# A two-layer trunk on one core: modulation weights of the prologue in x's buffers, the shift shared by two engines, attention ahead of the substitution, half norms issued later

## The chip, the core and the metric

The kernel runs on one core of a Trainium2 chip. The core has five engines, each with its own in-order queue: TensorE (matrix products; PE in the profile, with PEld for its weight loads), VectorE (DVE), ScalarE (ACT), GpSimd (POOL) and SyncE (SP), from whose queue most transfers are issued. They work on SBUF (128 partitions) and on PSUM, where products accumulate in a few banks. The metric is device time in microseconds (us) of one execution, lower is better. Three timed runs of the kernel before gave 2611.18, 2620.76 and 2622.28 us; the median is 2620.76.

## What is computed

The reference is a decoder trunk of two layers on a sequence of 1024 rows of 1024 numbers in float32, one sequence. Each layer has a mixer and a SwiGLU feed-forward part, and a conditioning vector `c` gives shift, scale and gate of each. Layer 0's mixer is a gated delta rule with 8 heads of 128 numbers, layer 1's is latent attention. The change touches layer 0's first norm and its mixer:

```
mod = silu(c) @ ada_w[0] + ada_b[0]               # shift_m, scale_m, gate_m, ...
h = rmsnorm(x, norm_mix_g[0]) * (1 + scale_m) + shift_m
proj = h @ w_in                                   # q, k, v, gate z, decay a, beta b of 8 heads
q, k, v = silu(causal_conv(q, k, v)); q, k = l2norm(q), l2norm(k)
per head, by chunks:
    A = I + strict_lower(beta k k^T * decay)      # solved against k and v
    attn = (q k^T) * decay
    S = S * g_last + k_dec^T v_new;  o = q_dec S + attn v_new
o = rmsnorm(o, norm_g) * silu(z)
x = x + gate_m * (o @ w_out)
```

Then follow the feed-forward part, layer 1 in the same manner, and a last norm.

## The kernel before, in words

One large product is done as three float32r products of high and low parts (`mm3`, L195 to L202), so every weight and every activation is split: ScalarE casts the high part (L177), VectorE subtracts for the low one (L178). The program's text is a list of tile operations; a scheduler turns it into one in-order list for each engine. It takes what is ready by the text's order of priority and counts a tile as free when all its readers are done, so the position in the text and the number of buffers of a pool decide where an operation lands. Pools have `bufs` buffers for each name.

The prologue (`gdn_prologue`, L543 to L624) loads the eight row tiles of `x` (`xin`), norms and transposes them to `xT` (L604 to L611), and computes the columns `cols[1]` (scale) and `cols[0]` (shift) in two halves of 512 columns (`ada`, L562 to L602). A half takes four transfers of 512 KB for the scale and four for the shift, each into a buffer `raw` of two blocks of rows. VectorE multiplies and adds the eight blocks into `acc` (L582, L584) and TensorE sums `acc` over the partitions with a column of ones (L588); the second half's shift goes to TensorE alone instead (`on_pe`, L579). From these come `A`, `neg` and the modulated rows `hThi` (L597) and `hTlo` (L601), through `d`, which has the name `xin` too (L599, L600). The first head's K and Q projections follow (L647): 48 products for each half of the rows of `hT`, into four PSUM banks.

Then comes the loop over heads, written by hand as a string of steps (L685): K projects k and q, V projects v and z, A prepares `L` (beta k k^T with decay), B solves and computes the attention, R is the recurrence. While head h is in R, head h+1 is solved (B) and head h+2 is projected and its `L` prepared (K, A, V).

- B, `gdn_prep_b` (L403): ScalarE gathers the diagonal blocks into `Ld`, VectorE transposes them to `Lr` (L414), does 31 substitution steps of two operations each (`st` L421, `X` L423), and transposes back to `Xn` (L425). Then the attention `at` for two groups of four chunks: a decay `decT` (`gdn_decay`, L344: GpSimd, TensorE L355, ScalarE L357, GpSimd L359), four products of K and Q (L433) and a multiply by VectorE (L434). At last the blocks are joined to `U` (L435 to L472).
- R, `gdn_rec` (L475): eight chunks, one after the other. A chunk transposes k and v (L488, L489), multiplies the state `S` by k and q (L496, L497), forms the residual `r` (L499), multiplies by `U` (L506) to `y`, feeds the state (L511, L515) and the output row `on` (L518, L520), and ScalarE sums its squares (L524). After four chunks the half is normed (L526 to L541): `t` (L527, L529), the power -1/2 on GpSimd (`rpow`, L219, result `co`), the scaling of `on` (L532), four transposes (L537), the gate (L539) and the store to HBM.

Names that return below: `pj` is the PSUM tile of a projection, `wraw`, `whi` and `wlo` a weight as loaded and its two parts, `cacc` the convolution.

Of the kernel before, what the change touches and what calls it, by code (L numbers as in the profile page):

```python
# [9 lines left out]
F32 = mybir.dt.float32  # L10
# [4 lines left out]
ALU = mybir.AluOpType  # L15
# [4 lines left out]
P = 128  # L20
T = 1024
D = 1024
NT = T // P
KT = D // P
H = 8
FF = 2816
NF = FF // P
EPS = 1e-6
# [4 lines left out]
class Trunk:  # L33
# [369 lines left out]
    def gdn_prep_b(self, h, kq, pr):  # L403

        nc, v = self.nc, self.nc.vector
        K, Q, L = kq["KT"], kq["QT"], pr["L"]
        M, R8 = NT, 32 // NT

        Ld = self.gw.tile([P, 32, M], F32, name="Ld")
        for b in range(4):  # L410
            pb = slice(b * 32, b * 32 + 32)
            nc.scalar.copy(Ld[pb], L[pb, :, b * 32:b * 32 + 32].rearrange("p m j -> p j m"))
        Lr = self.gw.tile([P, 32, 32], F32, name="Lr")
# [10 lines left out]
        Xn = self.gw.tile([P, 8, R8, M], F32, name="Xn")  # L424
        v.transpose(out=Xn.rearrange("p c r m -> p c (r m)"), in_=X.rearrange("p i c -> p c i"))  # L425
        U = self.gb.tile([P, M, P], F32, name="U", bufs=2)
        at = self.gb.tile([P, M, P], F32, name="at", bufs=2)
        for qd in range(2):
            dec = self.gdn_decay(h, qd, True, "decT")
            pa = self.pc.tile([P, 4, P], F32, name="c")  # L430
            for i in range(4):
                cs = slice((qd * 4 + i) * P, (qd * 4 + i + 1) * P)
                nc.tensor.matmul(pa[:, i], K[:, cs], Q[:, cs], start=True, stop=True)  # L433
            v.tensor_tensor(out=at[:, qd * 4:qd * 4 + 4], in0=pa, in1=dec, op=ALU.mult)  # L434
# [40 lines left out]
    def gdn_rec(self, h, kq, pr):  # L475
# [4 lines left out]
        for half in range(2):  # L480
            on = self.gw.tile([P, 4, P], F32, name="on")
            ss = self.gs.tile([P, 4], F32, name="ss")
            for cc in range(4):
# [10 lines left out]
                if c > 0:  # L494
                    pks = self.pd.tile([P, 2, P], F32, name="d")
                    nc.tensor.matmul(pks[:, 0], K[:, cs], S, start=True, stop=True)  # L496
                    nc.tensor.matmul(pks[:, 1], Q[:, cs], S, start=True, stop=True)  # L497
                    r = self.gw.tile([P, P], F32, name="r", bufs=2)
                    v.scalar_tensor_tensor(out=r, in0=pks[:, 0], scalar=c2[:, c:c + 1], in1=vs,  # L499
                                           op0=ALU.mult, op1=ALU.add)  # L500
                    qs = self.gw.tile([P, P], F32, name="qs", bufs=2)
                    nc.scalar.activation(out=qs, in_=pks[:, 1], func=AF.Copy, scale=self.eg[:, g:g + 1])
                else:
                    r = vs
# [16 lines left out]
                else:  # L521
                    v.tensor_copy(on[:, cc], po)
                junk = self.gw.tile([P, P], BF16, name="junk2")
                nc.scalar.activation(out=junk, in_=on[:, cc], func=AF.Square, accum_out=ss[:, cc:cc + 1])  # L524

            t1 = self.gs.tile([P, 4], F32, name="t1")  # L526
            v.tensor_scalar(out=t1, in0=qq[:, half * 4:half * 4 + 4], scalar1=EPS, scalar2=P * EPS, op0=ALU.add,  # L527
                            op1=ALU.mult)
            v.scalar_tensor_tensor(out=t1, in0=ss, scalar=1.0 / P, in1=t1, op0=ALU.mult, op1=ALU.add)  # L529
            co = self.gs.tile([P, 4], F32, name="co")  # L530
            self.rpow(co, t1)
            v.tensor_tensor(out=on, in0=on, in1=co.rearrange("p (c o) -> p c o", o=1).broadcast_to([P, 4, P]),  # L532
                            op=ALU.mult)
            sl = slice(half * 512, half * 512 + 512)
            pt = self.pd.tile([P, 4, P], F32, name="d")
            for i in range(4):
                nc.tensor.transpose(pt[:, i], on[:, i], self.ident)  # L537
            oT = self.gw.tile([P, 512], F32, name="oT")
            v.scalar_tensor_tensor(out=oT, in0=pt.rearrange("p a b -> p (a b)"), scalar=self.ggdn, in1=Z[:, sl],  # L539
                                   op0=ALU.mult, op1=ALU.mult)  # L540
            nc.sync.dma_start(out=self.o_dram[:, h, sl], in_=oT)  # L541

    def gdn_prologue(self, hi, lo):  # L543
# [7 lines left out]
        with ExitStack() as st:  # L551
            pool = st.enter_context(self.tc.tile_pool(name="n1", bufs=2))
            xs = [pool.tile([P, D], F32, name="xin", bufs=8) for _ in range(NT)]
# [8 lines left out]
            def ada(half):  # L562

                for m in (1, 0):
                    pc = bank([P, 4])
                    on_pe = half == 1 and m == 0
                    if not on_pe:
                        acc = pool.tile([P, 512], F32, name="acc", bufs=2)
                    for b in range(4):
                        raw = pool.tile([P, 2, 512], F32, name="raw", bufs=5)  # L570
                        o = m * D + half * 512
                        nc.sync.dma_start(out=raw, in_=a["ada_w"][0, b * 256:(b + 1) * 256, o:o + 512]
                                          .rearrange("(b p) n -> p b n", p=P))
                        for i in range(2):
                            kt = 2 * b + i
                            c = self.cact[:, kt:kt + 1]
                            if on_pe:
                                for ct in range(4):
                                    nc.tensor.matmul(pc[:, ct:ct + 1], raw[:, i, ct * P:(ct + 1) * P], c,  # L579
                                                     start=(kt == ct == 0), stop=(kt == KT - 1 and ct == 3))  # L580
# [5 lines left out]
                    if not on_pe:  # L586
# [9 lines left out]
                for kt in range(half * 4, half * 4 + 4):  # L596
                    nc.scalar.activation(out=hi[:, kt], in_=xT[:, kt], func=AF.Identity, scale=A[:, kt:kt + 1],  # L597
                                         bias=cols[0][:, kt:kt + 1])
                    d = pool.tile([P, D], F32, name="xin", bufs=8)  # L599
# [26 lines left out]
    def gdn(self, right, outer):  # L626
# [5 lines left out]
        with ExitStack() as s2:  # L632
# [21 lines left out]
            self.gs = s2.enter_context(tc.tile_pool(name="gs", bufs=2))  # L654
            self.xs = self.gw.tile([P, 4, P], F32, name="Xs")
# [17 lines left out]
            def do(tok):  # L673
# [7 lines left out]
                if k == "G":  # L681
                    gate = self.gate_row(0, 2, self.gq_pool, "KT", 3)
                    self.pre = gate, self.out_w((0, 1), a["gdn_w_out"][0], gate)
                if k == "R" and h < H - 1: self.gdn_rec(h, kqv[h], pr[h])
            pre, loop, tail = "A0 V0 B0 K1 A1 V1", "B1 R0 K2 A2 V2", "B6 R5 K7 A7 V7 G0 B7 R6"  # L685
            for t in pre.split():
                do(t)
            for h in range(H - 1):
# [8 lines left out]
                if h in (2, 4):  # L697
# [4 lines left out]
                         lambda: self.gdn_rec(H - 1, kqv[H - 1], pr[H - 1]))  # L702
# [805 lines left out]
```

## Time and profile before

| What | Value |
|---|---|
| Median of three timed runs | 2620.76 us (2611.18 to 2622.28) |
| The profiled execution's own time | 2613.28 us |
| Its span in the profile | 2611.6 us |
| TensorE busy, share of the span | 2505.5 us, 96% |
| TensorE weight loads | 2058.1 us, 79% |
| VectorE busy | 1962.5 us, 75% |
| ScalarE busy | 1173.5 us, 45% |
| GpSimd busy | 171.5 us, 7% |
| Read from HBM, written | 247.16 MB, 78.14 MB |

The profile is that of one execution. Ends of pipelined products are modelled, so a busy TensorE is not one at its peak; the starts are the firmer numbers. PEclk is the granted clock of TensorE as a share of full speed (0.50 is 1.2 GHz, 1.00 is 2.4 GHz). The prologue ends near 76 us, the linear-attention stage near 752 us, where the output projection's rows begin.

### The profile page before, as it was taken

How to read it: one execution, taken by the hardware profiler on the slowest of the kernel's cores; microseconds unless marked ns; L12 is line 12 of the kernel's file. 1: busy time of each engine (PE TensorE's matmuls, PEld its weight loads, DVE VectorE, ACT ScalarE, POOL GpSimd, SP SyncE). 2: the span in 40 equal slices, each digit the busy share in tenths (PEclk: the TensorE clock that was granted, in tenths of full speed). 3: DMA queues.
4: the chain of work that ended last, by engine and by line, in shares of the span. 5: the costliest groups of instructions: out<-in, count | busy, mean ns of one | idle time of the engine just before them, and what ended most of it. 6: DMA issues, size and time to landing. Idle time of an engine off the chain costs nothing.

```text
span 2611.6 us, 35555 instructions
## 1 busy us (share of the span) xinstructions
PE 2505.5 (96%) x12757; PEld 2058.1 (79%) x12757; DVE 1962.5 (75%) x3748; ACT 1173.5 (45%) x2374; POOL 171.5 (7%) x322
## 2 busy tenths in 40 slices
PE   6999999999999999999999899999999999999998
PEld 5777777777778888888888798888779888887886
DVE  5787789888758888877586766668577777774778
ACT  5555454555465222322344665555283332332343
POOL 1211111221000000000000010000010000000000
PEclk8999999999999999999999999999999999999999
DMA  6111222331454544544945521112643332336634
GB/s 228 41 33 33 75 79 85 89 102 62 153 181 142 182 153 155 160 147 156 314 146 153 155 70 60 47 51 87 216 157 96 108 108 93 108 104 224 226 94 145
DMA packets 258705, 327.62 MB, mean 125 GB/s; under 512 B 17578, under 2 KB 176448, under 8 KB 258528
## 3 DMA queue, kind: packets, MB, share of 16 engines
q1 hardware_dynamic: 235840, 284.37, 34.7%
q10 hardware_dynamic: 22688, 40.97, 4.2%
q8 instruction: 101, 1.65, 0.3%
q14 instruction: 76, 0.62, 0.1%
HBM read 247.16 MB, written 78.14 MB: 125 GB/s over the span
## 4 chain that ended last, share of the span: by engine, by line
PE 77%; DVE 11%; ACT 4%; DMA 3%; issue 2%; POOL 2%; ACTq 0%; POOLq 0%; DVEq 0%; SPq 0%
PE pd L971 14%; PE nrm_p L202 14%; PE pj L202 14%; PE pd L202 10%; PE P L202 8%; PE pd L1288 3%; PE po L202 2%; DVE cacc L334 2%; PE pq L202 1%; PE tp L1331 1%; DVE X L423 1%; DVE st L421 1%; ACT Xs L441 1%; DVE wlo L178 1%; PE d L511 1%
## 5 line engine op out<-in xcount | busy, mean ns | idle before, releaser
L971 PE MATMUL pd<-wlo,gh 128*128 128x512 f32 x616 | 243.9, 396 | 2.5 <-DVE wlo L178 2.0
L971 PE MATMUL pd<-whi,gl 128*128 128x512 f32 x616 | 241.3, 393 | 0.9 <-DVE gl L178 0.9
L971 PE MATMUL pd<-whi,gh 128*128 128x512 f32 x616 | 236.9, 394 | 3.7 <-ACT gh L177 3.3
L202 PE MATMUL pj<-hThi,whi 128*128 128x512 f32 x480 | 197.0, 410 | 0.0
L202 PE MATMUL pj<-hThi,wlo 128*128 128x512 f32 x480 | 196.5, 409 | 0.0
L202 PE MATMUL pj<-hTlo,whi 128*128 128x512 f32 x480 | 196.0, 408 | 0.0
L177 ACT CAST gh<-wraw 128x1024 fp32r<-128x1024 f32 x84 | 82.3, 979 | 247.4 <-PE pd L971 209.2
L177 ACT CAST whi<-wraw 128x1024 fp32r<-128x1024 f32 (+3 forms) x105 | 100.8, 961 | 143.8 <-DMA wraw<-in_ffn_w_gate_dram 54.2
L178 DVE TENSOR_TENSOR gl<-wraw,gh 128x1024 fp32r<-128x1024 f32 x84 | 95.2, 1133 | 63.9 <-ACT gh L177 63.4
L971 PEld LDWEIGHTS pd<-wlo,gh 128*128 128x128 f32 x616 | 116.3, 189 | 33.3 <-DVE wlo L178 8.1
L219 POOL TENSOR_TENSOR nrm_r<-nrm_r,mh 128x1 f32<-128x1 f32 x56 | 37.4, 669 | 1585.3 <-DVE nrm_r L213 965.7
L971 PEld LDWEIGHTS pd<-whi,gh 128*128 128x128 f32 x616 | 116.2, 189 | 30.4 <-ACT gh L177 4.2
L178 DVE TENSOR_TENSOR wlo<-wraw,whi 128x1024 fp32r<-128x1024 f32 (+3 forms) x105 | 117.5, 1119 | 28.6 <-ACT whi L177 26.4
L971 PEld LDWEIGHTS pd<-whi,gl 128*128 128x128 f32 x616 | 116.3, 189 | 26.6 <-DVE gl L178 1.5
L202 PE MATMUL nrm_p<-T,xrow 128*128 128x512 f32 (+1 forms) x576 | 133.7, 387 | 0.0
L202 PE MATMUL nrm_p<-T,ow_hi 128*128 128x512 f32 (+1 forms) x600 | 132.0, 369 | 0.0
L202 PE MATMUL nrm_p<-T,ow_lo 128*128 128x512 f32 (+1 forms) x552 | 125.8, 376 | 0.0
L202 PEld LDWEIGHTS nrm_p<-T,xrow 128*128 128x128 f32 x576 | 105.3, 189 | 23.5
L202 PEld LDWEIGHTS nrm_p<-T,ow_hi 128*128 128x128 f32 x600 | 103.8, 189 | 20.6 <-ACT fh L791 0.2
L202 PEld LDWEIGHTS nrm_p<-T,ow_lo 128*128 128x128 f32 x552 | 98.0, 189 | 20.4
L334 DVE SCALAR_TENSOR_TENSOR cacc<-cr,cwc,cacc 128x512 f32<-128x512 f32 x144 | 108.5, 760 | 3.3 <-ACT cacc L332 2.8
L202 PEld LDWEIGHTS pj<-hTlo,whi 128*128 128x128 f32 x480 | 92.0, 192 | 15.4
(531 smaller groups left out, 6399.0 us busy)
## 6 DMA issues: line engine op xcount, KB each, us to landing
wraw<-in_ada_w_dram SPq DMA_DIRECT2D x80, 512.0 KB, 4.1
wraw<-in_ffn_w_gate_dram SPq DMA_DIRECT2D x44, 512.0 KB, 3.9
wraw<-in_ffn_w_up_dram SPq DMA_DIRECT2D x44, 512.0 KB, 4.4
gd_S<-sx ACTq DMA_DIRECT2D x88, 256.0 KB, 2.5
B<-in_ffn_w_down_dram SPq DMA_DIRECT2D x40, 512.0 KB, 6.8
wraw<-gd_S SPq DMA_DIRECT2D x40, 512.0 KB, 5.1
gd_A<-co ACTq DMA_DIRECT2D x66, 256.0 KB, 2.1
wraw<-in_gdn_w_in_dram SPq DMA_DIRECT2D x32, 512.0 KB, 4.6
```

The source lines that it names most:

```text
L177: nc.scalar.copy(hi, raw)
L178: nc.vector.tensor_tensor(out=lo, in0=raw, in1=hi.bitcast(F32), op=ALU.subtract)
L202: nc.tensor.matmul(out, l, r, start=(i == 0), stop=(i == len(seq) - 1))
L219: self.nc.gpsimd.tensor_tensor(out=out, in0=in_, in1=self.mh[:, 0:in_.shape[1]], op=ALU.pow)
L334: nc.vector.scalar_tensor_tensor(out=acc, in0=cr[:, j:j + 512], scalar=self.cw[:, j, ch:ch + 1], in1=acc, op0=ALU.mult, op1=ALU.add)
L421: v.tensor_tensor(out=t[:, 0:n], in0=Lr[:, j, j + 1:32].rearrange("p (i o) -> p i o", o=1).broadcast_to([P, n, 8]), in1=X[:, j:j + 1].broa ...
L423: v.tensor_tensor(out=X[:, j + 1:32], in0=X[:, j + 1:32], in1=t[:, 0:n], op=ALU.subtract)
L441: nc.scalar.copy(Xs[pb, :, b * 32:b * 32 + 32].rearrange("p m (r c) -> p m r c", c=8), Xn[pb, :, :, mh].rearrange("p c r m -> p m r c"))
L511: nc.tensor.matmul(psn, kd, y, start=True, stop=True)
L971: nc.tensor.matmul(acc[t], x[:, j, ts], y[:, j], start=(j0 + j == 0 and k == 0), stop=(j0 + j == NJ - 1 and k == 2))
L1288: nc.tensor.matmul(sc[:, 0:nm], q[:, ts], k[:, cs], start=(i == 0), stop=(i == 4 and not last))
L1331: nc.tensor.transpose(pt[:, kt - k0], pes[qi][:, kt * P:(kt + 1) * P], self.ident)
```

## The change

There are four edits, all in layer 0's first part.

1. The prologue's modulation weights lose their own buffers (`raw`, five) and are loaded under the name `xin`, which now has sixteen buffers instead of eight.
2. The shift is summed by both engines in both halves: even blocks of rows by VectorE into `acc`, odd ones by TensorE straight into PSUM, to which the product of `acc` with ones is added.
3. In B, the attention block stands ahead of the transposition to `Lr` and of the substitution instead of behind them; `Xn` takes the buffer `Ld`.
4. The norm of a half becomes a function of its own, `gdn_half`. The recurrence only notes the finished half; the norm is issued after the second chunk of the next half, or at a new step E of the string. `on` gets two buffers instead of one and `qs` one instead of two.

```diff
@@ gdn_prep_b
+        U = self.gb.tile([P, M, P], F32, name="U", bufs=2)
+        at = self.gb.tile([P, M, P], F32, name="at", bufs=2)
+        for qd in range(2):
+            dec = self.gdn_decay(h, qd, True, "decT")
+            pa = self.pc.tile([P, 4, P], F32, name="c")
+            for i in range(4):
+                cs = slice((qd * 4 + i) * P, (qd * 4 + i + 1) * P)
+                nc.tensor.matmul(pa[:, i], K[:, cs], Q[:, cs], start=True, stop=True)
+            v.tensor_tensor(out=at[:, qd * 4:qd * 4 + 4], in0=pa, in1=dec, op=ALU.mult)
         Lr = self.gw.tile([P, 32, 32], F32, name="Lr")
...
-        Xn = self.gw.tile([P, 8, R8, M], F32, name="Xn")
+        Xn = self.gw.tile([P, 32, M], F32, name="Ld").rearrange("p (c r) m -> p c r m", r=R8)
...
@@ gdn_rec
-            on = self.gw.tile([P, 4, P], F32, name="on")
+            on = self.gw.tile([P, 4, P], F32, name="on", bufs=2)
...
-                    qs = self.gw.tile([P, P], F32, name="qs", bufs=2)
+                    qs = self.gw.tile([P, P], F32, name="qs")
...
                 nc.scalar.activation(out=junk, in_=on[:, cc], func=AF.Square, accum_out=ss[:, cc:cc + 1])
-
-            t1 = self.gs.tile([P, 4], F32, name="t1")
...
+                if cc == 1:
+                    self.gdn_half()
+            self.gdn_end = (h, half, on, ss, qq, Z)
+
+    def gdn_half(self):
+
+        if self.gdn_end is None:
+            return
+        nc, v = self.nc, self.nc.vector
+        h, half, on, ss, qq, Z = self.gdn_end
+        self.gdn_end = None
+
+        t1 = self.gs.tile([P, 4], F32, name="t1")
...
@@ gdn_prologue
-            xs = [pool.tile([P, D], F32, name="xin", bufs=8) for _ in range(NT)]
+            xs = [pool.tile([P, D], F32, name="xin", bufs=16) for _ in range(NT)]
...
-                        raw = pool.tile([P, 2, 512], F32, name="raw", bufs=5)
+                        raw = pool.tile([P, D], F32, name="xin", bufs=16).rearrange("p (b n) -> p b n", b=2)
...
-                            if on_pe:
+                            if m == 0 and i == 1:
                                 for ct in range(4):
                                     nc.tensor.matmul(pc[:, ct:ct + 1], raw[:, i, ct * P:(ct + 1) * P], c,
-                                                     start=(kt == ct == 0), stop=(kt == KT - 1 and ct == 3))
+                                                     start=(kt == 1 and ct == 0), stop=False)
...
-                    if not on_pe:
-                        for ct in range(4):
-                            nc.tensor.matmul(pc[:, ct:ct + 1], acc[:, ct * P:(ct + 1) * P], self.ones[:, 0:1],
-                                             start=True, stop=True)
+                    for ct in range(4):
+                        nc.tensor.matmul(pc[:, ct:ct + 1], acc[:, ct * P:(ct + 1) * P], self.ones[:, 0:1],
+                                         start=(m == 1), stop=(m == 1 or ct == 3))
...
@@ gdn
+                if k == "E": self.gdn_half()
                 if k == "R" and h < H - 1: self.gdn_rec(h, kqv[h], pr[h])
-            pre, loop, tail = "A0 V0 B0 K1 A1 V1", "B1 R0 K2 A2 V2", "B6 R5 K7 A7 V7 G0 B7 R6"
+            pre, loop, tail = "A0 V0 B0 K1 A1 V1", "B1 R0 K2 E0 A2 V2", "B6 R5 K7 E0 A7 V7 G0 B7 R6 E0"
...
-                         lambda: self.gdn_rec(H - 1, kqv[H - 1], pr[H - 1]))
+                         lambda: (self.gdn_rec(H - 1, kqv[H - 1], pr[H - 1]), self.gdn_half()))
```

Lines of the kernel after are shifted: L655 is the first projections' product (L647 before), L605 and L608 the modulated rows (L597, L600), L540, L543 and L548 the norm's `t`, scaling and transposes (L529, L532, L537), L430 and L432 the substitution's steps (L421, L423).

How the engines' queues move is shown at three places. First ScalarE's list in the prologue, from the last copy of `xT` on, before:

```order
L611 COPY xT<-d 128x512
L177 CAST whi<-wraw 128x1024
L597 ACTIVATE hThi<-xT,col_0_161,Am_162 128x1024 x2
L600 ACTIVATE xin<-hThi,neg 128x1024 x2
L597 ACTIVATE hThi<-xT,col_0_161,Am_162 128x1024 x2
L600 ACTIVATE xin<-hThi,neg 128x1024 x2
L177 CAST whi<-wraw 128x1024
L597 ACTIVATE hThi<-xT,col_0_161,Am_162 128x1024 x2
```

And the same place after:

```order
L619 COPY xT<-d 128x512
L605 ACTIVATE hThi<-xT,col_0_161,Am_162 128x1024 x2
L608 ACTIVATE xin<-hThi,neg 128x1024 x2
L605 ACTIVATE hThi<-xT,col_0_161,Am_162 128x1024 x2
L608 ACTIVATE xin<-hThi,neg 128x1024 x2
L177 CAST whi<-wraw 128x1024 x2
L605 ACTIVATE hThi<-xT,col_0_161,Am_162 128x1024 x2
```

The cast of the first projection weight moved from ahead of the first modulated rows to behind all four of that half.

Second TensorE's list in head 2's recurrence, from the last projection products of the first half to the next chunk's products with the state, before:

```order
L202 MATMUL pj<-hThi,whi 128x512
L202 MATMUL pj<-hTlo,whi 128x512
L202 MATMUL pj<-hThi,wlo 128x512
L537 MATMUL d<-ident,on 128x128 x4
L488 MATMUL d<-ident,KT 128x128
L489 MATMUL d<-ident,VT 128x128
L202 MATMUL pj<-hThi,whi 128x512
L202 MATMUL pj<-hTlo,whi 128x512
L202 MATMUL pj<-hThi,wlo 128x512
L202 MATMUL pj<-hThi,whi 128x512
L496 MATMUL d<-S,KT 128x128
L497 MATMUL d<-S,QT 128x128
```

A chunk without the norm in a recurrence after, from the output row of one chunk to the next one's products with the state:

```order
L518 MATMUL d<-y,at 128x128
L202 MATMUL pj<-hThi,wlo 128x512
L202 MATMUL pj<-hThi,whi 128x512
L488 MATMUL d<-ident,KT 128x128
L489 MATMUL d<-ident,VT 128x128
L202 MATMUL pj<-hTlo,whi 128x512
L496 MATMUL d<-S,KT 128x128
L497 MATMUL d<-S,QT 128x128
```

At the half boundary the four transposes of the normed half, and the run of projection products ahead of them, no longer stand between one chunk and the next; two to five products do.

Third VectorE's list around the scaling (the `on` from `on` and `co`) of the same half of head 2, before:

```order
L515 SCALAR_TENSOR_TENSOR S<-S,eg_820,d 128x128
L423 TENSOR_TENSOR X<-X,st 128x48
L520 TENSOR_TENSOR on<-d,qs 128x128
L421 TENSOR_TENSOR st<-Lr,X 128x40
L334 SCALAR_TENSOR_TENSOR cacc<-cr,cwc,cacc 128x512
L423 TENSOR_TENSOR X<-X,st 128x40
L529 SCALAR_TENSOR_TENSOR t_2829<-ss,t_2829 128x4
L334 SCALAR_TENSOR_TENSOR cacc<-cr,cwc,cacc 128x512
L421 TENSOR_TENSOR st<-Lr,X 128x32
L532 TENSOR_TENSOR on<-on,co 128x512
```

And after:

```order
L499 SCALAR_TENSOR_TENSOR r<-d,c_1439,vs 128x128
L430 TENSOR_TENSOR st<-Lr,X 128x24
L540 SCALAR_TENSOR_TENSOR t_2888<-ss,t_2888 128x4
L432 TENSOR_TENSOR X<-X,st 128x24
L338 SCALAR_TENSOR_TENSOR KT<-KT,cacc 128x512
L430 TENSOR_TENSOR st<-Lr,X 128x16
L543 TENSOR_TENSOR on<-on,co 128x512
L432 TENSOR_TENSOR X<-X,st 128x16
L515 SCALAR_TENSOR_TENSOR S<-S,eg_825,d 128x128
```

The scaling stood behind the half's last update of the state and its output row; now it stands between the residual `r` of a later chunk and that chunk's update of `S`.

## Rows read from the trace of the kernel before

**Rows 1.** The page's first line.

```profile
span 2611.6 us, 35555 instructions
```

**Rows 2.** Windows: start:end, length, busy us and instructions by engine, granted clock, transfers.

```profile
core 0: us, PE busy (x) PEld busy (x) DVE busy (x) ACT busy (x) POOL busy (x), PEclk, DMA share, GB/s
0.00:76.00 76.00, 51.00 (x256) 42.33 (x257) 47.67 (x101) 46.67 (x65) 8.24 (x50) 0.89 0.63 204
...
250.00:350.00 100.00, 91.71 (x513) 74.13 (x511) 85.16 (x209) 50.66 (x132) 20.63 (x26) 0.97 0.27 79
```

**Rows 3.** Timeline, VectorE in the prologue: start, us, engine, line, operation, count.

```profile
30.78 4.69 DVE L584 SCALAR_TENSOR_TENSOR acc<-raw,cact,acc 128x512 f32<-128x512 f32 x6
...
64.00 2.47 DVE L601 SCALAR_TENSOR_TENSOR hTlo<-xT,Am,xin 128x1024 fp32r<-128x1024 f32 x2
```

**Rows 4.** Timeline, ScalarE in the prologue.

```profile
37.75 2.37 ACT L597 ACTIVATE hThi<-xT,col,Am 128x1024 fp32r<-128x1024 f32 x2 [1.81 <-DVE col L591]
...
44.37 2.18 ACT L600 ACTIVATE xin<-hThi,neg 128x1024 f32<-128x1024 f32 x2
...
60.18 2.37 ACT L597 ACTIVATE hThi<-xT,col,Am 128x1024 fp32r<-128x1024 f32 x2 [12.69 <-DVE Am L593]
```

**Rows 5.** Timeline, TensorE in the prologue.

```profile
42.53 0.79 PE L647 MATMUL pj<-hTlo,whi 128*128 128x512 f32 x1 [2.27 <-DVE hTlo L601]
...
47.22 1.84 PE L579 MATMUL d<-cact,raw 128*128 128x1 f32 x16
...
58.77 0.95 PE L588 MATMUL e<-ones,acc 128*128 128x1 f32 x8
...
64.94 0.62 PE L647 MATMUL pj<-hThi,whi 128*128 128x512 f32 x2
...
75.93 0.39 PE L202 MATMUL pj<-hThi,whi 128*128 128x512 f32 x1
```

**Rows 6.** Chain of waits, an undisturbed run of projection products.

```profile
555.40 13.30 PE pj L202 x58
```

**Rows 7.** Timeline, TensorE's products with U in heads 2 and 5, and the transposes.

```profile
271.41 0.46 PE L506 MATMUL d<-r,U 128*128 128x128 f32 x2
...
274.89 0.46 PE L506 MATMUL d<-r,U 128*128 128x128 f32 x2
...
280.27 0.66 PE L537 MATMUL d<-ident,on 128*128 128x128 f32 x4 [0.62 <-DVE on L532]
...
283.20 0.46 PE L506 MATMUL d<-r,U 128*128 128x128 f32 x2
...
509.70 0.46 PE L506 MATMUL d<-r,U 128*128 128x128 f32 x2
...
519.01 0.38 PE L506 MATMUL d<-r,U 128*128 128x128 f32 x2
```

**Rows 8.** Waits of TensorE, 150 to 752 us: total us, times, longest.

```profile
PE c L433 <- DVE at L434: 12.8, 5, 4.7
PE d L537 <- DVE on L532: 6.1, 10, 0.8
```

**Rows 9.** Waits of VectorE, 150 to 752 us.

```profile
DVE on L532 <- POOL co L219: 10.4, 11, 1.2
```

**Rows 10.** Timeline, VectorE: a substitution step near head 2's attention.

```profile
261.89 0.33 DVE L423 TENSOR_TENSOR X<-X,st 128x168 f32<-128x168 f32 x1
```

**Rows 11.** Windows: two stretches at half clock, as in rows 2.

```profile
261.60:268.40 6.80, 5.53 (x21) 5.14 (x22) 5.40 (x16) 1.99 (x7) 0.63 (x1) 0.50 0.25 77
...
654.10:660.90 6.80, 5.30 (x20) 4.67 (x21) 5.90 (x13) 2.62 (x7) 1.49 (x1) 0.50 0.55 186
```

**Rows 12.** The tile co (ns: min/median/max), and a scaling in VectorE's timeline.

```profile
L219 POOL TENSOR_TENSOR co<-t,mh x16: 1006/1019/1955, 199.2 to 736.5; 128x4 f32<-128x4 f32 x16
...
279.52 0.69 DVE L532 TENSOR_TENSOR on<-on,co 128x512 f32<-128x512 f32 x1 [0.90 <-POOL co L219]
```

**Rows 13.** Timeline, ScalarE: one of the prologue's table loads.

```profile
69.01 1.28 ACT L1101 ACT_TABLE_LOAD   x1
```

More of the change, by code (lines that the diff above doesn't have):

```diff
@@ L423, in gdn_prep_b @@
             v.tensor_tensor(out=X[:, j + 1:32], in0=X[:, j + 1:32], in1=t[:, 0:n], op=ALU.subtract)
-        Xn = self.gw.tile([P, 8, R8, M], F32, name="Xn")
+        Xn = self.gw.tile([P, 32, M], F32, name="Ld").rearrange("p (c r) m -> p c r m", r=R8)
         v.transpose(out=Xn.rearrange("p c r m -> p c (r m)"), in_=X.rearrange("p i c -> p c i"))
[L426 to L434, printed above, removed]
         for m0 in range(0, M, 4):
@@ L524, in gdn_rec @@
                 nc.scalar.activation(out=junk, in_=on[:, cc], func=AF.Square, accum_out=ss[:, cc:cc + 1])
-            t1 = self.gs.tile([P, 4], F32, name="t1")
[L527 to L540, printed above, removed]
@@ L541, in gdn_rec @@
-            nc.sync.dma_start(out=self.o_dram[:, h, sl], in_=oT)
+                if cc == 1:
[8 more added lines that the diff above has]
+        t1 = self.gs.tile([P, 4], F32, name="t1")
+        v.tensor_scalar(out=t1, in0=qq[:, half * 4:half * 4 + 4], scalar1=EPS, scalar2=P * EPS, op0=ALU.add,
+                        op1=ALU.mult)
+        v.scalar_tensor_tensor(out=t1, in0=ss, scalar=1.0 / P, in1=t1, op0=ALU.mult, op1=ALU.add)
+        co = self.gs.tile([P, 4], F32, name="co")
+        self.rpow(co, t1)
+        v.tensor_tensor(out=on, in0=on, in1=co.rearrange("p (c o) -> p c o", o=1).broadcast_to([P, 4, P]),
+                        op=ALU.mult)
+        sl = slice(half * 512, half * 512 + 512)
+        pt = self.pd.tile([P, 4, P], F32, name="d")
+        for i in range(4):
+            nc.tensor.transpose(pt[:, i], on[:, i], self.ident)
+        oT = self.gw.tile([P, 512], F32, name="oT")
+        v.scalar_tensor_tensor(out=oT, in0=pt.rearrange("p a b -> p (a b)"), scalar=self.ggdn, in1=Z[:, sl],
+                               op0=ALU.mult, op1=ALU.mult)
+        nc.sync.dma_start(out=self.o_dram[:, h, sl], in_=oT)
@@ L565, in ada @@
                     pc = bank([P, 4])
-                    on_pe = half == 1 and m == 0
-                    if not on_pe:
-                        acc = pool.tile([P, 512], F32, name="acc", bufs=2)
+                    acc = pool.tile([P, 512], F32, name="acc", bufs=2)
                     for b in range(4):
-                        raw = pool.tile([P, 2, 512], F32, name="raw", bufs=5)
+                        raw = pool.tile([P, D], F32, name="xin", bufs=16).rearrange("p (b n) -> p b n", b=2)
                         o = m * D + half * 512
@@ L585, in ada @@
                                                        op1=ALU.add)
-                    if not on_pe:
-                        for ct in range(4):
-                            nc.tensor.matmul(pc[:, ct:ct + 1], acc[:, ct * P:(ct + 1) * P], self.ones[:, 0:1],
-                                             start=True, stop=True)
+                    for ct in range(4):
+                        nc.tensor.matmul(pc[:, ct:ct + 1], acc[:, ct * P:(ct + 1) * P], self.ones[:, 0:1],
+                                         start=(m == 1), stop=(m == 1 or ct == 3))
                     hs = slice(half * 4, half * 4 + 4)
@@ L598, in ada @@
                                          bias=cols[0][:, kt:kt + 1])
-                    d = pool.tile([P, D], F32, name="xin", bufs=8)
+                    d = pool.tile([P, D], F32, name="xin", bufs=16)
                     nc.scalar.activation(out=d, in_=hi[:, kt].bitcast(F32), func=AF.Identity, bias=neg[:, kt:kt + 1])
@@ L654, in gdn @@
             self.gs = s2.enter_context(tc.tile_pool(name="gs", bufs=2))
+            self.gdn_end = None
             self.xs = self.gw.tile([P, 4, P], F32, name="Xs")
```

## The prediction

> **What bounds the kernel now.** I began with the two builds' instruction orders: from the end of the linear-attention stage on, the rows of all five engines are the same, so only the first 752 us of the 2611.6 us span [rows 1] can move. The windows came next [rows 2]: in the prologue (0 to 76 us) no engine is full (TensorE 51.00 of 76) and transfers run at 204 GB/s; in the stage's loop TensorE shows 91.71 us of 100 busy and VectorE 85.16, both near full and neither full. The reader is to see two coupled in-order queues: a stall in one is partly filled by the other. Then I read the prologue's timeline [rows 3 to 5], the recurrence around a half boundary [rows 6, 7], and the waits of TensorE and VectorE over 150 to 752 us [rows 8, 9].
>
> A normal chunk of the recurrence takes 274.89 - 271.41 = 3.48 us from one product with `U` to the next. A chunk at a half boundary takes 283.20 - 274.89 = 8.31 in head 2 and 519.01 - 509.70 = 9.31 in head 5 [rows 7], mean 8.8: there the power on POOL, the scaling on VectorE and four transposes (from 280.27, after 0.62 us idle) stand in TensorE's queue ahead of the next chunk. The time is not empty: by the order, fourteen or fifteen projection products stand before the transposes.
>
> **The change part by part.** *Prologue.* The same sixteen transfers of 512 KB are fetched. The shift's four even blocks of rows go to VectorE and the four odd ones to TensorE, in both halves. First half: eight multiply-adds become four. The last six before took 4.69 us, 0.78 each [rows 3]; four fewer is 3.1 us, plus some 0.6 of waiting inside the longer run, so the first modulated row (37.75 [rows 4]) starts near 34. Then the order decides. Before, ScalarE rounds the first projection weight ahead of the modulated rows; after, both weight casts stand behind all eight of those operations. These take 44.37 + 2.18 - 37.75 = 8.8 us [rows 4], so the first product waits until 34 + 8.8 + one cast of 1.0 = 43.8. Before, TensorE's products ran from 42.53 on [rows 5]. The 3.7 us gained are spent, and 1.3 more.
>
> Second half: the shift is now half on VectorE, and its closing product stands in TensorE's queue behind all 48 products of the first half. From 43.8 I add 48 products at 0.229 (13.30 / 58 [rows 6]) = 11.0; two groups of shift products at 1.84 [rows 5], where four stood in this stretch, = 3.7; two closing groups of 0.95 [rows 5] = 1.9; and 2.7 because the first dozen still run at half clock, at twice 0.229. This gives 63.1, and with the adds behind it the second half's rows start at 63.4 instead of 60.18 [rows 4]. Before, TensorE had products of the first half until 64.94 [rows 5] and saw no gap; now its queue is empty. VectorE's first low part ended at 64.00 + 1.24 = 65.2, 5.0 after that start [rows 3, 4]; now it ends at 68.4, and the 44 products behind it end at 68.4 + 44 x 0.229 = 78.5, where the next projection began at 75.93 [rows 5]. With a short stretch at half clock behind the gap: **+3 us**. Bounds: -4 (the early start survives) and +5. That all weights are fetched ahead I price at nothing: by the 34 us above they have landed, and the queues in front of their users are longer.
>
> *Attention ahead of the substitution.* The text moves it ahead of the 31 substitution steps. In the orders it hardly moves: TensorE still meets these products behind the next head's V projection (57 to 69 products before, 48 to 74 after). In heads 1, 3, 4 and 5 VectorE has one to three fewer substitution pairs in front of the first `at`, some 0.7 us a pair (a step there 0.33 [rows 10]); in head 7 two more. TensorE's waits for `at` are 12.8 us in five places [rows 8]. I take 1.4 off in three of them: **-4 us**. Bounds: 0, and all 12.8 with the two stretches at half clock behind the longest waits (6.8 each, granted clock 0.50 [rows 11], half of which is lost), -19.6.
>
> *Half norms later.* The same instructions, moved: the norm of a half is issued after the second chunk of the next half, or at the points E of the schedule. A boundary chunk on TensorE holds 23 products (5.3), four transposes (0.5) and some 1.3 us of small products (by the starts in a normal chunk): 7.1 of 8.8, 1.7 lost. A normal chunk holds eight (1.8) and 1.3: 3.1 of 3.48, 0.4 lost. The difference, 1.3 us at eight first boundaries, is 10.4. At the eight ends of a head other products stand ready, and I give these only 1 for what is left of the 6.1 us wait for the scaled half [rows 8], and 2 for the last head's shorter tail: **-13.5 us.** What is late next: VectorE. The scaling now stands between the residual `r` and the update of the state `S`, on the recurrence itself. It waits for POOL's power, 1.019 us median, with one to four short operations as cover, and takes 0.69 itself [rows 12]. Queued behind it are the update and, through it, TensorE's next two products with `S`. In front of these TensorE has some four to eight projection products, four transposes and two more, about 2.7 us, so a delay of 0.8 to 1.7 is covered; uncovered it costs up to 16 x 1.7 = 27. Bounds: -42, if the 5.3 us by which a boundary exceeds a normal chunk vanished eight times, and +27. I take the value nearest to the boundary rows, as each end needs all places to fall one way. The single `qs` buffer costs nothing: its reader stands right behind the update, ahead of the next chunk's writer; were it late, up to eight chunks of each head would wait a fraction of a microsecond. Of the table loads two fall away, 1.28 each [rows 13], beside waits of ScalarE: nothing, and at most -2.6.
>
> Sum: 3 - 4 - 13.5 = -14.5 us on the profiled execution's own 2613.28 us: 2598.8. That execution is 7.5 us below the median of the three timed runs (2620.76) and 2.1 above their lowest; I add half of the 7.5 for where a new median would lie: **2602.5 us**.
>
> **Rivals.** *Larger gain.* The waits for `at` go too, with their half-clock stretches: 19.6 instead of 4, so 2587. For it: these are the longest single waits, up to 4.7 [rows 8]. Against it: the orders leave the products where they were.
>
> *No change.* VectorE is the real bound: with 85 us of 100 busy [rows 2] and the same instructions, what TensorE gains at the boundary comes back as a wait for VectorE elsewhere. The prologue's +3 stays and the loop gives 0: 2613.3 + 3 + 3.7 = 2620. For it: VectorE's wait for the power, 10.4 us in eleven places [rows 9], stays, as little stands between the power and its user. Against it: 15 us in 100 of VectorE are idle.
>
> *Slower: the norm sits on the recurrence.* At each of the 16 norms the state's update waits for power and scaling. This decides from the point where the delay passes the 2.7 us that TensorE holds ready, or where the recurrence and not TensorE's stream sets the pace. Price: 16 x 1.7 = 27, less the 8 x 1.1 that the boundaries save beyond their products, prologue +5: +23, so 2640. For it: the power has run up to 1.955 us [rows 12]; at that length the delay reaches 2.6. Against it: the median is 1.019. The Trainium skill (GPSIMD Engine Reference, section Key points) says that GpSimd shares its SBUF interfaces with VectorE and contends with VectorE instructions that have two SBUF inputs; the substitution's steps are such, and the deferred power runs among them. The spread from 1.006 to 1.955 [rows 12] agrees with a contention; by that rule the long value would be the usual one and the time this rival's, by the median row it is the forecast's.
>
> **How the numbers follow.** Forecast 0.45, own range 2592 to 2612; larger gain 0.17; no change 0.26; slower 0.12. What a measurement can tell from no change is 0.5%, 13 us: below 2607.7 or above 2633.9. Faster: 0.36 of the forecast's 0.45, all of the larger gain, 0.01 of no change: 0.54. Slower: 0.11, most of the last rival. Within: 0.35. The range leaves out about half of each outer rival: 2582 to 2625.
>
> **What the profile will show.** Right: boundary chunks of 3.5 to 4.5 us from one product with `U` to the next; TensorE's wait for the scaled half near 0; the prologue's first product near 44, ScalarE's second batch of rows near 63, the next projection near 78.5; waits for `at` of some 9 us; the stage's end near 737 instead of 752. Wrong: a first product before 41 (the cast was not the gate); VectorE's wait for the power well over 10.4 with TensorE idle behind a late `S` (the slower rival); boundaries gone but the stage's end unmoved, with new waits at the V projection or behind the substitution (no change).

## The result, and the profile after

The kernel after takes 2643.18 us, the median of 13 runs (2624.76 to 2646.66), beside 2621.24 for the kernel before: the ratio is 1.008, interval 1.0063 to 1.0097. It is slower by 22 us, where 18 us less had been forecast.

The profiled execution took 2624.76 us and was the shortest of the thirteen; eight took 2643 to 2647. This profile therefore holds only part of the loss, and is read first for what it does show. Its span is 2623.0 us. Two stretches of 676 us follow, the loop over heads after and the same length before (columns as in [rows 2]; the x counts are instructions):

```profile
85.00:761.00 676.00, 638.23 (x3527) 505.14 (x3526) 552.90 (x1452) 350.39 (x914) 118.30 (x160) 0.98 0.27 81
```

```profile
76.00:752.00 676.00, 638.48 (x3522) 506.77 (x3521) 552.54 (x1451) 349.02 (x911) 117.21 (x159) 0.98 0.27 81
```

The loop gives next to nothing back: the same busy time and, within five, the same number of TensorE instructions in 676 us. From the first product of the next projection to the first one of the output projection's rows it takes 674.3 us after (86.6 to 760.9) and 675.9 before (75.9 to 751.8). What this profile loses lies ahead of the loop, 10.7 us, and, by two stretches at half clock that are 3.4 us longer and one that is new, behind it, some 2.3 us.

**The prologue after**, by ScalarE's, TensorE's and VectorE's timelines (start, us, engine, line, operation):

```profile
24.19 0.30 ACTq L1079 DMA_DIRECT2D pi<-in_positions_dram  x1
...
39.29 2.37 ACT L605 ACTIVATE hThi<-xT,col,Am 128x1024 fp32r<-128x1024 f32 x2 [7.76 <-DVE col L599]
...
47.98 1.97 ACT L177 CAST whi<-wraw 128x1024 fp32r<-128x1024 f32 x2
69.21 2.38 ACT L605 ACTIVATE hThi<-xT,col,Am 128x1024 fp32r<-128x1024 f32 x2 [19.26 <-DVE col L599]
```

```profile
33.14 4.15 PE L588 MATMUL d<-cact,xin 128*128 128x1 f32 x26
37.15 1.84 PE L596 MATMUL d<-ones,acc 128*128 128x1 f32 x8
49.06 0.79 PE L655 MATMUL pj<-hThi,whi 128*128 128x512 f32 x1 [10.07 <-ACT whi L177]
...
86.59 0.39 PE L202 MATMUL pj<-hThi,whi 128*128 128x512 f32 x1
```

```profile
28.87 0.22 DVE L1081 CAST pf<-pi 8x128 f32<-8x128 int32 x1 [2.08 <-DMA pi<-in_positions_dram]
```

Against [rows 4, 5]: the first rows start at 39.29 instead of 37.75, the first product at 49.06 (bulk at 42.53 before), the second half's rows at 69.21 instead of 60.18, the next projection at 86.59 instead of 75.93.

**The half boundary after**, TensorE's products with `U` in head 2 (against [rows 7]), then the last one of head 2 and the first of head 3; below them the same pair before:

```profile
282.57 0.46 PE L506 MATMUL d<-r,U 128*128 128x128 f32 x2
286.07 0.46 PE L506 MATMUL d<-r,U 128*128 128x128 f32 x2
290.13 0.46 PE L506 MATMUL d<-r,U 128*128 128x128 f32 x2
...
309.60 0.38 PE L506 MATMUL d<-r,U 128*128 128x128 f32 x2
350.02 0.38 PE L506 MATMUL d<-vs,U 128*128 128x128 f32 x2
```

```profile
303.94 0.38 PE L506 MATMUL d<-r,U 128*128 128x128 f32 x2
340.38 0.39 PE L506 MATMUL d<-vs,U 128*128 128x128 f32 x2
```

The boundary chunk is 290.13 - 286.07 = 4.06 us where it was 8.31. But from one recurrence to the next it is now 40.42 us where it was 36.44: projection products that left the recurrence stand there (130 in this stretch, 113 before; the boundary chunk has 11 instead of 23). TensorE's waits over 150 to 762 us after (us, times, longest), and the row of before that answers to the second:

```profile
PE c L420 <- DVE at L421: 15.1, 7, 4.6
PE e L447 <- DVE U L443: 6.2, 4, 2.4
PE d L548 <- DVE on L543: 2.8, 4, 1.0
PE d L488 <- DVE S L515: 2.2, 6, 0.5
```

```profile
PE e L447 <- DVE U L443: 3.4, 3, 2.2
```

The wait for the scaled half fell from 6.1 [rows 8] to 2.8; waits for `S` (2.2) and for `U` (2.8 more) came, and those for `at` rose from 12.8 [rows 8] to 15.1. All of TensorE's waits from 76 to 762 us add up to 37.1 us in both profiles.

### The profile page after: what moved, and what is told of

It is laid out like the page before. It is cut to its first block, busy times and chain, and to the rows that moved or that the text cites. A ratio compares the mean times of both kernels' runs of the same rounds, so it can differ in the third digit from the quotient of the medians.

```text
span 2623.0 us, 35565 instructions
## 1 busy us (share of the span) xinstructions
PE 2511.0 (96%) x12765; PEld 2060.2 (79%) x12765; DVE 1960.9 (75%) x3748; ACT 1170.7 (45%) x2372; POOL 172.2 (7%) x322
## 4 chain that ended last, share of the span: by engine, by line
PE 78%; DVE 11%; ACT 4%; DMA 4%; issue 2%; POOL 2%; SPq 0%; ACTq 0%; POOLq 0%; DVEq 0%
PE pd L981 15%; PE nrm_p L202 14%; PE pj L202 14%; PE pd L202 10%; PE P L202 8%; PE pd L1298 3%; PE po L202 2%; PE pq L202 1%; DVE cacc L334 1%; PE tp L1341 1%; DVE wlo L178 1%; DVE st L430 1%; DVE X L432 1%; ACT Xs L441 1%; PE pj L655 1%
```

## Where the other 20 us are: a second profile of the kernel after

The kernel was run again, unchanged, beside its parts.

> The kernel after, unchanged, timed beside its parts. Every theory expects a ratio near 1.008 to the kernel before. What it is to tell: the profiled execution after took 2624.76 us and was the fastest of thirteen, most took some 2645. If the 20 us between are stretches at half clock, a profile of a slower execution shows 40 us more at 0.50 than the first profile, and shows in which stage.

Measured: 2645.0 us, ratio 1.0072 (1.0044 to 1.0100). The profiled execution took 2648.7. Two stretches at the same times in both profiles, first the shorter execution's, then this one's (PEclk, the granted clock, is the third number from the end; in the second stretch the shorter execution is 7 us ahead in its work):

```profile
178.10:202.00 23.90, 22.32 (x146) 17.89 (x146) 16.37 (x35) 12.69 (x32) 4.19 (x6) 0.93 0.08 23
239.50:263.40 23.90, 23.90 (x131) 19.57 (x131) 17.93 (x55) 11.00 (x31) 3.52 (x6) 1.00 0.11 32
```

```profile
178.10:202.00 23.90, 23.90 (x102) 19.59 (x102) 10.06 (x17) 10.12 (x21) 5.31 (x6) 0.50 0.09 23
239.50:263.40 23.90, 23.90 (x108) 20.04 (x108) 11.12 (x38) 7.79 (x23) 2.24 (x3) 0.50 0.12 34
```

Twice 23.9 us passed at 1.2 GHz. The order of instructions is the same, and so are the waits at the two joins: TensorE's first product with `U` of heads 1 and 2, at the joins at the end of B (h = 0 and 1 in the code). They are, in the shorter execution and in this one:

```profile
177.14 1.10 PE L447 MATMUL e<-U,L 128*128 128x64 f32 x8 [2.38 <-DVE U L443]
231.55 1.10 PE L447 MATMUL e<-U,L 128*128 128x64 f32 x8 [1.92 <-DVE U L443]
```

```profile
177.41 1.37 PE L447 MATMUL e<-U,L 128*128 128x64 f32 x8 [2.36 <-DVE U L443]
238.89 1.42 PE L447 MATMUL e<-U,L 128*128 128x64 f32 x8 [1.91 <-DVE U L443]
```

In the first, half clock lasted 3.4 us from 178.2 and 3.4 from 232.8; in the second 23.9 and 23.9. The second execution has 54.7 us more at half clock in all (130.7 against 76.0 by the profile's clock, counted behind 30 us), half of which is 27, and is 24 us longer.

Each run also tells its mean granted clock. From it comes a second number for each kernel: the run's time less (1 - clock) x span, which counts half of each stretch at 1.2 GHz as lost. It is rough (the clock is given to 0.001, 2.6 us, and a stretch in which TensorE waits costs less), but it parts the two causes. Below, medians; "full-clock" is the mean of that number over the runs. The ratio is to runs of the kernel before in the same session, so it is no quotient of these medians.

| Kernel | runs | us | ratio to before (interval) | clock | full-clock us |
|---|---|---|---|---|---|
| before | 107 | 2621 | | 0.984 | 2579 |
| after (both rows of runs) | 19 | 2644 | 1.008, 1.0072 | 0.977 | 2583 |
| p_only: prologue alone | 12 | 2622 | 1.0009 (0.9995 to 1.0022) | 0.986 | 2584.5 |
| h_only: half norms alone | 12 | 2621.5 | 0.9991 (0.9977 to 1.0006) | 0.984 | 2579 |
| a_only: attention ahead alone | 12 | 2614 | 0.9993 (0.9974 to 1.0013) | 0.986 | 2577 |
| ha: half norms and attention | 12 | 2624 | 1.0017 (0.9998 to 1.0037) | 0.984 | 2581 |
| ph: prologue and half norms | 12 | 2629 | 1.0022 (1.0008 to 1.0037) | 0.982 | 2583 |
| pa: prologue and attention | 12 | 2627 | 1.0028 (1.0013 to 1.0042) | 0.982 | 2581 |

So the loss is some 4 us of work and waits and some 19 of clock: (0.984 - 0.977) x 2640 = 18.5. In the two profiles above the same reckoning gave 27 where the times differ by 24, so the clock's part may be nearer 16 and the rest nearer 6. No single edit has it.

## The experiments

**One edit or two at a time.** Each kernel is the kernel before with parts of the diff shown above.

```diff
 p_only   edits 1 and 2        ha   edits 3 and 4
 h_only   edit 4 (Xn in Ld)    ph   edits 1, 2 and 4
 a_only   edit 3               pa   edits 1, 2 and 3
```

> The kernel before with the changed prologue alone. Theory 1 (the loss is the prologue: in the trace after, its next projection starts some 9 us late, and the loop gives nothing back): ratio 1.004 to 1.008, next projection near 85 us instead of 75.93. Theory 2 (the norm on the recurrence, in the loop, makes the loss): 1.000 to 1.002.

> The kernel after with the prologue of before: attention ahead and half norms later, without the first two edits. Theory 1: ratio 0.997 to 1.002, so the loop's edits are worth nothing. Theory 2: 1.004 to 1.008. The prediction's sum without its prologue term: 0.993.

> The kernel before with the half norms alone (prologue and the attention's place as before; Xn in the buffer Ld, as after). Theory 1: 0.997 to 1.002, boundary chunks near 4 us but the stage's end unmoved. Theory 2: 1.004 to 1.008. The prediction's term: 0.995.

> The kernel after with the attention back behind the substitution (prologue and half norms as after). Theory 3 (the loss is half clock: TensorE's wait of 2.4 us for U at head 1's join and a new one of 1.9 at head 2's let the clock fall, and in most executions it then stays down through the whole join, 23.9 us each time, as a second profile of the kernel after shows): the wait at head 2's join comes with the attention's new place, so this kernel has at most one long stretch: ratio 0.999 to 1.003. Rival (the prologue's 10 us simply come on top of the loop's edits): 1.004 to 1.008.

> The kernel after with the norms of before (prologue and attention ahead of the substitution as after). Theory 3: the wait of some 1.9 us at head 2's join and a long stretch at half clock stay, ratio 1.003 to 1.008. Rival (the norms between r and the update of S lose the time): 1.000 to 1.003.

> The kernel before with the attention ahead of the substitution alone. The prediction's term: 0.9985. Theory 3: 1.000 to 1.004, with the wait at head 2's join in the profile and single slower executions with a clock below 0.980.

Theory 1 falls: the next projection starts at 88.2 in p_only, and yet the kernel is no slower by a measurable amount. Part of the reason is that before's own prologue is not always done at 76: in h_only, which has it unchanged, a stretch of 20.5 us at half clock began at 52.5 and the next projection started at 85.7; in a_only and ha at 76.8 and 76.7. Theory 2 falls with h_only and ha. Theory 3 stands in ph. The profiles of ph and pa have one long stretch each, 23.9 us from 177.8 and 177.7, at head 1's join, and each ratio is between those of the single edits and of all. In pa it missed: the ratio, 1.0028, lies just under its range and inside the rival's, and the wait of 1.9 us that I expected is 0.72. It missed in a_only too, with 0.9993 and the same wait of 0.72. The executions of two kernels fall in two groups: a_only has eight of 2608 to 2616 us at clocks of 0.985 and more and four of 2627 to 2629 at 0.979 to 0.981, ha eight of 2618 to 2626 at 0.983 and more and four of 2631 to 2639 at 0.977 to 0.981. Only executions of the shorter groups were profiled.

The wait of 1.9 us at head 2's join belongs to edits 3 and 4 together: 1.91 in ha, 0.72 in a_only and pa, none in h_only. VectorE's rows there, first in the second profile after, then in h_only, show why:

```profile
234.08 0.16 DVE L432 TENSOR_TENSOR X<-X,st 128x8 f32<-128x8 f32 x1
235.06 0.69 DVE L543 TENSOR_TENSOR on<-on,co 128x512 f32<-128x512 f32 x1 [0.82 <-POOL co L219]
235.67 0.67 DVE L434 STREAM_TRANSPOSE Ld<-X 128x256 f32<-128x256 f32 x1
```

```profile
227.06 0.68 DVE L425 STREAM_TRANSPOSE Ld<-X 128x256 f32<-128x256 f32 x1
...
229.50 0.69 DVE L543 TENSOR_TENSOR on<-on,co 128x512 f32<-128x512 f32 x1 [0.92 <-POOL co L219]
```

With both edits the scaling of head 1's second half, and its wait for POOL, stand between the last substitution step and the transposition on which the join waits; with the half norms alone they stand behind it.

**Work in the waits.** Five products that nothing reads, ahead of the first product with `U`:

```diff
+            if m0 == 0 and h in (0, 1): [nc.tensor.matmul(pw..., self.ident, Xn..., start=True, stop=True) for _ in range(5)]
```

> The kernel after with five products of 256 columns that nothing reads, issued ahead of the first product with U at the joins of heads 1 and 2, where TensorE waited 2.4 and 1.9 us; the planned order changes with them. Theory 3: the clock does not fall there, or comes back at once: no stretch of 20 us at half clock, and although work is added the ratio falls from 1.0075 to 0.999 to 1.003. Rival (the clock is only a mark of the slower executions, not their cause): the added products cost 2 to 4 us and the ratio is 1.007 to 1.010.

Measured: 1.0049 (1.0031 to 1.0067), 2631.9 us, the median of six. TensorE no longer waits for `U` at head 1's join, but 1.62 us of idle time, for `Xn` in the buffer `Ld`, stand ahead of the added products (x10 for five: two instructions each). No stretch of 23.9 us is in the profile:

```profile
174.87 2.43 PE L444 MATMUL e<-Ld,ident 128*128 128x256 f32 x10 [1.62 <-DVE Ld L434]
177.39 1.10 PE L447 MATMUL e<-U,L 128*128 128x64 f32 x8
```

Half clock still came at 185.1, for 13.7 us; head 2's join had none. The kernel is 12 us shorter than after by the medians, 6 to 8 by the ratios, although its full-clock time is 6 longer (2589). The ratio lies between the ranges of theory 3 and of its rival: the direction is theory 3's, its size was missed. The added products and an order that changed with them are not told apart here.

**Shorter waits, no work added.** Half of the copies to `Xs` go to VectorE, which waits for them there; in s0 and s1 in one head only.

```diff
-                nc.scalar.copy(Xs[pb, ...], Xn[pb, :, :, mh]...)
+                (nc.scalar.copy if b < 2 else v.tensor_copy)(Xs[pb, ...], Xn[pb, :, :, mh]...)
```

> The kernel after with the copies to Xs shared: of the four blocks ahead of each transposition to U, two go from ScalarE to VectorE, which waits there for ScalarE. It shortens the chain in front of TensorE's first product with U by some 0.8 us and adds no work. Theory 3 (these waits let the clock fall at the joins of heads 1 and 2, and the long stretches are the loss): waits for U at these joins below 1.5 us, ratio 0.998 to 1.003 where the kernel after has 1.0075. Rival (the copies load VectorE, which bounds the loop): 1.0075 or more.

> The kernel after with the copies to Xs shared for head 1 alone. Theory 3 (the kernel after loses two long stretches at half clock, some 10 us each, one at the join of head 1 and one at that of head 2): with only the first wait shortened one of the two goes: median between 2630 and 2640, ratio 1.003 to 1.006. Rival (only the second, which needs both edits, costs): no change, 1.0075.

> The kernel after with the copies to Xs shared for head 2 alone. Theory 3: the stretch at head 2's join goes, that at head 1's stays: median between 2630 and 2640, ratio 1.003 to 1.006, and the profile shows at most one stretch of 23.9 us. Rival (the shared copies help through the shorter chains of all eight heads, not through the clock): 1.007.

Measured: after_split 1.0031 (1.0014 to 1.0047), 2626.2 us; s0 1.0052 (1.0031 to 1.0073), 2638.1; s1 1.0049 (1.0033 to 1.0066), 2631.7. The waits at the two joins in after_split, the stretch and the second wait in s1, and both stretches in s0:

```profile
177.35 1.10 PE L447 MATMUL e<-U,L 128*128 128x64 f32 x8 [1.93 <-DVE U L443]
230.62 1.10 PE L447 MATMUL e<-U,L 128*128 128x64 f32 x8 [1.47 <-DVE U L443]
```

```profile
178.50:202.40 23.90, 23.90 (x103) 19.59 (x102) 9.94 (x18) 10.12 (x21) 4.84 (x5) 0.50 0.09 23
...
239.17 1.10 PE L447 MATMUL e<-U,L 128*128 128x64 f32 x8 [1.46 <-DVE U L443]
```

```profile
176.10:199.90 23.80, 23.80 (x102) 19.48 (x102) 10.61 (x19) 9.41 (x20) 5.47 (x6) 0.50 0.08 23
237.50:261.40 23.90, 23.90 (x108) 19.98 (x107) 11.12 (x38) 7.72 (x23) 2.24 (x3) 0.50 0.12 34
```

With 0.45 us less wait at the two joins the median is 18 us lower (2644 to 2626), by the ratios 11 to 13. The full-clock time stays near after's (2584.6 beside 2583), so what was won is clock: 0.985 beside 0.977. The ratio, 1.0031, lies just above my range and far from the rival's. One place gives part: in s1 the second join's stretch is gone and the first's stays; in s0, whose first wait is still 1.94 us, seven runs of twelve (2637 to 2644) look like after, five (2623 to 2630) do not, and its profile is of the first kind. Both have after's full-clock time (s0 2583, s1 2583.5), and the intervals of both ratios touch after's. The waits fell less than the 0.8 us expected, to 1.93 and 1.47 and not below 1.5 both. At head 1's join the length of the wait does not decide by itself: the same 1.93 or 1.94 us were followed by 3.4 us at half clock in after_split's profile and by 23.9 in that of s0. That the shorter wait itself keeps the clock up there is not shown.

**The two halves of the prologue**, one profile each:

```diff
 p_share: raw keeps its own buffers       p_buf: the shift is summed as before
-raw = ...name="xin", bufs=16)            -if m == 0 and i == 1:
+raw = ...name="raw", bufs=5)             +if on_pe:
```

> The kernel before with the shared shift alone, the weights in their own five buffers. If the share makes the prologue longer (both casts behind the rows, the second half's rows behind all products): second half's rows some 4 us late against before, first product later than 44. If it is the buffers (positions fetched late, VectorE waits for them): the prologue is within 2 us of before.

> The kernel before with the weights in x's buffers alone, the shift summed as before. If the buffers make the prologue longer, VectorE waits some 2 us for the positions, and the first product starts that much later than 42.5; if it is the share, the prologue is within 2 us of before.

Single runs: 2617.1 and 2629.4 us, too few for a ratio. Next projection at 83.0 and 87.8. Rows of VectorE, TensorE and ScalarE, first p_share's first modulated rows with the last weights' arrival ahead of them, then those of p_buf:

```profile
35.23 0.75 DVE L582 SCALAR_TENSOR_TENSOR acc<-raw,cact,acc 128x512 f32<-128x512 f32 x1 [1.11 <-DMA raw<-in_ada_w_dram]
36.91 1.84 PE L585 MATMUL d<-ones,acc 128*128 128x1 f32 x8
39.05 1.24 ACT L594 ACTIVATE hThi<-xT,col,Am 128x1024 fp32r<-128x1024 f32 x1 [7.79 <-DVE col L588]
```

```profile
28.50 0.21 DVE L1071 CAST pf<-pi 8x128 f32<-8x128 int32 x1 [1.56 <-DMA pi<-in_positions_dram]
41.08 1.24 ACT L597 ACTIVATE hThi<-xT,col,Am 128x1024 fp32r<-128x1024 f32 x1 [10.44 <-DVE col L591]
```

Neither expectation alone is right: both prologues are longer. The share puts the casts behind the rows (first product 48.8) and gives no earlier rows, as the last weights and TensorE's own products are then late; the buffers move the fetch of the positions from 6 to some 24 us on ScalarE's queue, and VectorE waits for it. How much of the loss each half holds is not shown: with an unchanged prologue the next projection started anywhere from 75.9 to 86.5 us in single profiles (before, h_only, a_only, ha and a_split below).

**A version from the best parts.** a_split is a_only with the shared copies; pas is a_split with p_share's prologue.

```diff
 a_split: edit 3, shared copies to Xs
 pas:     edits 2 and 3, shared copies to Xs
```

> The attention ahead of the substitution alone (prologue and norms of before), with the same shared copies. If the long stretch of its slower executions (2627 to 2629 beside 2608 to 2616) hangs on the wait for U at head 1's join, all executions come out between 2600 and 2617: ratio 0.994 to 0.998, faster than before and after. Rival: no change to the attention alone, 0.999, with both groups of executions.

> A version put together from the parts: the shift shared by two engines with the weights in their own buffers, attention ahead of the substitution, shared copies to Xs, norms as before. By the parts (full-clock time 2574 for the attention with shared copies, 2.5 for the shared shift, half of 66 us at half clock as in the profile of the shared shift): 2610, ratio 0.994 to 0.998. Rival (the edits' places against the clock's falls decide, not the sum): 0.999 to 1.004.

Measured: 0.999 (0.9971 to 1.0008) and 0.9994 (0.9978 to 1.0010): neither beats before, and both lie in the ranges of the rivals. The full-clock times are low (2575 and 2576, for pas what the sum gave), but half clock stayed: a stretch of 13.7 us at head 1's join in a_split's profile, of 20.5 in pas's, where the wait is still 1.94 in both. That fits the rival by which the places of the clock's falls decide and not the sum.

## Why the prediction was wrong

Two steps failed, and together they are most of the miss. One is the gain of the half norms, -13.5, which measured 0 (h_only). The other is the clock. The sum had -4, -13.5 and +3 us of work and waits, with half clock as a part of the waits for `at` alone, and "a short stretch" in the prologue; the row that should have warned was there, TensorE's longest wait for `U` in the profile before, at head 1's join, with 6.8 us at half clock behind it from 169.4 on:

```profile
168.74 1.40 PE L447 MATMUL e<-U,L 128*128 128x64 f32 x8 [2.22 <-DVE U L443]
```

I took no price for such a stretch growing. It measured some 16 to 19 us by the runs' clocks; in the second profile after, the two joins hold 47.8 us at half clock where these 6.8 were.

- *Prologue, +3.* By full-clock time +5 (p_only). The order's part was right: the first product waited for all eight operations and one cast, 39.29 + 8.69 + 1.0 = 49.0, and the second half's rows stood behind all products. Wrong was the start "near 34": 39.29. The shift's products on TensorE were priced at nothing in the first half; 26 of their 32 instructions take 4.15 us ahead of the closing product, most of it at half clock (from 34.8 on). And of the queues past which a DMA moves I had not followed ScalarE's: the positions' fetch went out at 24.19 instead of 6, a wait of 2.08 us on VectorE. "That all weights are fetched ahead I price at nothing" failed there.
- *Attention ahead, -4.* By full-clock time -2, not measurable in the ratio. The reason given does not hold: waits for `at` are 12.8 us in a_only's profile too, as in [rows 8], and 15.1 in after's, where some 9 were forecast.
- *Half norms, -13.5.* By full-clock time 0. The places moved as forecast, boundary chunks from 8.3 to 4.1 us, the wait for the scaled half from 6.1 to 2.8. Mis-sized was the loss to be won: 1.3 us a boundary was the difference of two estimates (1.7 and 0.4, the latter from one chunk), while the rows showed only 0.62 us idle there. The products that left the boundary were issued elsewhere; 37.1 us of waits became 37.1.
- *The rivals.* "No change" has the loop right: what is gained at the boundary comes back as waits for `S`, `U` and `at`, and the stage ends at 761 us where 737 was forecast. "Slower: the norm sits on the recurrence" has the operation right and the place wrong: waits for `S` are 2.2 us in six places, but the scaling with its wait for POOL delayed the join. That its 2640 us lie near the measured 2643 is luck: its price, up to 1.7 us at each of 16 norms, did not come. VectorE's wait for the power did not grow: 10.2 us in eleven places in the first profile after, 10.4 in [rows 9]; the power's median is 1.176 us there and 1.030 in the second, 1.019 in [rows 12]. By the rule of the Trainium skill (GPSIMD Engine Reference, section Key points), contention on the shared SBUF interfaces, it would have grown. The 10.2 us do not bear that out.

Shown is that long stretches at half clock make most of the difference: two profiles of one order, and kernels with after's full-clock time (after_split, s0, s1) that lose less by as much as their clocks are higher. Shown too is that the wait at head 2's join needs edits 3 and 4 together; in the two profiles where it is shorter, 1.47 and 1.46 us, no half clock came behind it, though one profile each cannot say how often. Not settled is why the wait at head 1's join, 2.2 to 2.4 us in every kernel without shared copies there or added products, is followed by 3.4 or 6.8 us at half clock in the profiles of before, p_buf, p_only, h_only, a_only, ha and the first of after and by 23.9 in ph, pa, s1 and the second of after, though the prologue alone changes nothing near it. In p_share it is followed by none (a row of the timeline, and a window as in [rows 2]):

```profile
174.40 0.77 PE L447 MATMUL e<-U,L 128*128 128x64 f32 x5 [2.23 <-DVE U L443]
...
174.40:198.30 23.90, 23.90 (x169) 19.73 (x170) 21.11 (x60) 12.22 (x37) 5.65 (x7) 1.00 0.09 23
```

## What to carry to other kernels

Before pricing a gain from moving work off a spot, look at the idle time that the rows show there: here it was 0.62 us a boundary, and the work taken from between two others in a full queue only moved. Where the granted clock falls in a profile, look at each run's clock and at more than one profile before pricing an edit: the profiled execution can be the one that escaped. A wait of 2 us ahead of many small products deserves its own line in the sum, since what followed it here cost up to five times as much (23.9 us at half clock, half of which is 12).

## What the runs showed of the hardware

After waits of 1.9 to 2.4 us at one place, head 1's join, half clock lasted 3.4, 6.8, 13.7, 20.5 or 23.9 us or did not come, in two executions of one kernel 3.4 and 23.9. In 23.9 us at 0.50 TensorE issued 102 instructions there, at 0.93 it issued 146 and at 1.00 169 (the latter in p_share, whose order differs). At 0.50 it was shown busy throughout: the profile shows no idle time in the very stretch that came behind an idle wait.
